# Ready outputs of the first mixer split ahead of the memory projection, the memory projection's weight rests used last in a step, half a projection step ahead of two transposes

## The chip, the cores and the metric

One core of a Trainium2 chip runs the whole kernel. The metric is the device time of one execution in microseconds (us); the median of the runs before the change is 2076.57.

The engines have these names here: PE (TensorE, matmuls and transposes), DVE (VectorE), ACT (ScalarE), POOL (GpSimd) and SP (SyncE, which issues most transfers).

## The reference, cut to what matters

A hybrid encoder of two layers works on 512 positions of 1024 features. Each layer adds half a SwiGLU to its input, then the output of a mixer, then cross-attention to a memory of 256 rows, then half a second SwiGLU. What the change touches:

```
# mixer, layer 0: h @ w_in -> 8 heads with top-k keys (q, k normalised), 4 differential heads
#   logits = q.k + bias, masked; p = softmax; attn = p1 - lam * p2; o = rmsnorm(attn @ v)
# mixer, layer 1: h @ w_in -> 16 heads over a band of 9 chunks of 64
#   p = softmax(q.k + bias); o = p @ v
h = h + concat(o) @ w_out
# cross-attention, 4 heads of 128
k, v = split(rmsnorm(memory) @ mem_wkv)      # memory: 256 x 1024
h = h + softmax(norm(h' @ wq) . norm(k)) @ v @ wo
```

## The kernel before, in words

**Products.** Every fp32 product is made from two parts of each operand: `h`, the value rounded to the format that TensorE reads, and `l`, the rest. Three matmuls then add up: high by high, high by low, low by high. For weights ScalarE makes `wh` (line 161) from the landed `wf`, and VectorE or GpSimd makes `wl` (line 163). Which of the two makes it follows a table of shares: in layer 0's memory projection every second `wl` is GpSimd's, in layer 1's all are VectorE's. There are two buffers each of `wh` and `wl`. For the attention's outputs ScalarE makes `oh` (line 1327) and VectorE the rest `ol` (line 1329).

**Order of TensorE.** TensorE's order is written out by hand: a generator of projections and one of attention are woven together (`weave`, line 79). The attention yields gaps in ns, and the projections yield the cost of each piece; the weave pulls pieces until a gap is filled. The other engines' orders come from a scheduler that knows the dependencies, with some instructions held behind others by `behind` and `issue_after`. PSUM has eight banks: four with the tag `pa` for projections and four with `pb` for attention.

**A mixer.** Six chunks of the input projection come first (`gemm_nat`, matmuls in line 706). Their four banks are copied out by ScalarE (`raw`, line 731) and normalised per head. Then follows the memory projection (`mem_kv`, matmuls in line 1104): eight steps over the features, each of them 12 matmuls into four banks, two for the keys and two for the values. Within a step the banks come one after the other, and each gets `wh*mh`, `wl*mh` and `wh*ml` in a row; after the first two banks and after the last two it yields 1300. Its end empties the banks: keys by ScalarE (line 1110), values by ScalarE (the high part, line 1116) and then VectorE (the rest, line 1117). At last comes the output projection (`out_proj`, matmuls in line 657), which takes four banks of the tag `pa` and works through the outputs in steps of 12 matmuls.

Beside it runs the attention: transposes of queries and keys (lines 766 and 785, split by ScalarE in 775, 789 and 790, and VectorE in 776 and 791), logits (812), the exponentials with bias and maximum (DVE 825, ACT 826), transposes of the probabilities (837, split by ScalarE in 840 and by VectorE in 841 into pz0, pz1 and pz2), values (864 and 920), and the outputs' assembly (868, 869, 873, 874). In layer 0 the differential heads give the first outputs.

**Splitting the outputs.** `mix_out` hands `out_proj` a function `parts(k)`; it makes `oh` and `ol` of output k when it is first asked and the output is ready. It is asked when `out_proj` reaches step k.

**Cross-attention** (`xattn`, line 1163). Queries in line 1254; `soft` makes the logits (1196), the maxima (1199), the exponentials (1204) and their scaling (1211) of a head; `turn` makes eight transposes of a head's probabilities in two banks (1219), each split by ScalarE (1220) into pz0h or pz2h and by VectorE (1221) into pz0l or pz2l; `values` makes six matmuls (1231) and splits their result into `oh` (1234) and `ol` (1236), which are what the output projection of the cross-attention reads (line 657 again).

## Time and profile before

| what | value |
|---|---|
| median of 3 runs | 2076.57 us (2076.25 to 2076.64) |
| the profiled execution | 2077.4 us |
| its span | 2075.6 us |
| mean granted TensorE clock | 0.999 |
| busy: PE | 2045.8 us |
| busy: DVE | 1564.7 us |
| busy: ACT | 1136.6 us |
| busy: POOL | 361.7 us |

The span runs from the first to the last instruction that the profiler shows; the execution's own time is a little longer. A line of the timeline gives start and duration in us, the engine, the line in the kernel, the operation and its output and input; in brackets stands how long the engine was idle ahead of it, and what ended that. A line of the waits gives who waited for whom, the total in us, the number of times and the longest. A line of the windows gives, for a stretch of time, the busy time of PE, its weight loads, DVE, ACT and POOL with their number of instructions, and then the granted clock of TensorE, where 1.00 is full speed.

### The profile page before, as it was taken

The page shows a single profiled execution, that of the slowest core. Times are in us where ns is not written, and L with a number is a line of the kernel's source. Part 1 is how long each engine was busy: PE and PEld are TensorE (multiplying, and loading weights), DVE is VectorE, ACT ScalarE, POOL GpSimd, SP SyncE. Part 2 cuts the span into 40 slices and gives each one's busy share as a digit, 9 for nine tenths or more (in the row PEclk, how much of TensorE's full clock was granted, in tenths as well). Part 3 has the DMA queues.
Part 4 walks back from the last instruction along what each step waited for, and adds up shares of the span by engine and source line. Part 5 has one row for each costly group of instructions (what it writes and reads, how often), then busy time and mean ns, then how long its engine had stood idle before and what let it go on. Part 6 is the DMA issues. An engine that isn't in the chain of part 4 may idle for free.

```text
span 2075.6 us, 32512 instructions
## 1 busy us (share of the span) xinstructions
PE 2045.8 (99%) x12834; PEld 1825.3 (88%) x12834; DVE 1564.7 (75%) x2246; ACT 1136.6 (55%) x1701; POOL 361.7 (17%) x319
## 2 busy tenths in 40 slices
PE   8999999999999999999999999999999999999999
PEld 7989897888788889898989899988888888989997
DVE  8959687699676698685889687685668687958676
ACT  6636354556686565362556354454778566626442
POOL 1101003345431110000020000013453122000000
PEclk9999999999999999999999999999999999999999
DMA  7837545222241166573556466444223324647643
GB/s 218 221 113 193 142 115 180 82 87 82 83 137 61 62 184 172 143 192 113 128 158 176 129 182 164 122 126 149 92 82 125 100 72 141 184 122 182 164 120 94
DMA packets 86121, 279.65 MB, mean 135 GB/s; under 512 B 9680, under 2 KB 12880, under 8 KB 85968
## 3 DMA queue, kind: packets, MB, share of 16 engines
q1 hardware_dynamic: 74448, 235.62, 35.3%
q0 software_dynamic: 11520, 41.95, 11.8%
q8 instruction: 101, 1.65, 0.3%
q14 instruction: 52, 0.43, 0.1%
HBM read 271.24 MB, written 6.29 MB: 134 GB/s over the span
## 4 chain that ended last, share of the span: by engine, by line
PE 86%; DVE 9%; ACT 2%; issue 2%; POOL 1%; DMA 1%; SPq 0%; DVEq 0%; ACTq 0%; POOLq 0%
PE ps_pa L468 26%; PE ps_pa L604 10%; PE ps_pa L706 10%; PE ps_pb L604 10%; PE ps_pb L468 9%; PE ps_pa L657 4%; PE ps_pb L812 2%; PE ps_pa L323 2%; PE ps_pa L1254 2%; PE ps_pb L864 1%; PE ps_pa L1104 1%; PE ps_pb L657 1%; PE ps_pb L837 1%; DVE wl L163 1%; PE ps_pa L1023 1%
## 5 line engine op out<-in xcount | busy, mean ns | idle before, releaser
L161 ACT ACTIVATE wh<-wf 128x1024 fp32r<-128x1024 f32 (+2 forms) x211 | 215.3, 1022 | 345.9 <-PE ps_pa L604 122.1
L163 DVE TENSOR_TENSOR wl<-wf,wh 128x1024 fp32r<-128x1024 f32 (+2 forms) x169 | 200.0, 1188 | 32.5 <-ACT wh L161 29.9
L446 ACT ACTIVATE wh<-s 128x1024 fp32r<-128x1024 f32 x108 | 114.9, 1063 | 111.9 <-PE ps_pa L468 33.6
L525 POOL DMA_DIRECT2D s<-l_ffn_wq x40 | 35.4, 885 | 782.8 <-ACT s L524 739.0
L447 DVE TENSOR_TENSOR wl<-s,wh 128x1024 fp32r<-128x1024 f32 x108 | 132.0, 1222 | 44.3 <-ACT wh L446 40.1
L446 ACT ACTIVATE wh<-wf 128x1024 fp32r<-128x1024 f32 x84 | 89.2, 1062 | 105.9 <-PE ps_pa L468 32.6
L163 POOL TENSOR_TENSOR wl<-wf,wh 128x1024 fp32r<-128x1024 f32 x42 | 101.4, 2415 | 137.6 <-ACT wh L161 135.7
L706 PE MATMUL ps_pa<-wh,xh 128*128 128x512 f32 x384 | 122.8, 401 | 0.1
L706 PE MATMUL ps_pa<-wh,xl 128*128 128x512 f32 x384 | 119.4, 392 | 0.0
L706 PE MATMUL ps_pa<-wl,xh 128*128 128x512 f32 x384 | 119.1, 391 | 0.0
L447 DVE TENSOR_TENSOR wl<-wf,wh 128x1024 fp32r<-128x1024 f32 x84 | 102.5, 1220 | 5.5 <-PE ps_pa L323 3.0
L228 POOL TENSOR_TENSOR acc<-acc,sq 128x512 f32<-128x512 f32 (+1 forms) x37 | 53.0, 1433 | 260.7 <-ACT sq L227 259.7
L614 DVE TENSOR_TENSOR dn<-ps_pa,R 128x512 f32<-128x512 f32 x48 | 33.1, 689 | 83.9 <-PE ps_pa L604 83.5
L604 PE MATMUL ps_pb<-hh,wh 128*128 128x512 f32 x352 | 95.5, 389 | 0.0
L604 PE MATMUL ps_pb<-hl,wh 128*128 128x512 f32 x352 | 95.4, 389 | 0.0
L604 PE MATMUL ps_pb<-hh,wl 128*128 128x512 f32 x352 | 95.4, 389 | 0.0
L604 PE MATMUL ps_pa<-hh,wh 128*128 128x512 f32 x328 | 88.9, 390 | 0.0
L604 PE MATMUL ps_pa<-hl,wh 128*128 128x512 f32 x328 | 88.7, 389 | 0.0
L604 PE MATMUL ps_pa<-hh,wl 128*128 128x512 f32 x328 | 88.6, 389 | 0.0
L614 DVE TENSOR_TENSOR dn<-ps_pb,R 128x512 f32<-128x512 f32 x48 | 33.0, 687 | 71.1 <-PE ps_pb L604 70.7
L706 PEld LDWEIGHTS ps_pa<-wh,xl 128*128 128x128 f32 x384 | 72.5, 189 | 15.9
L706 PEld LDWEIGHTS ps_pa<-wl,xh 128*128 128x128 f32 x384 | 72.4, 188 | 15.8
(377 smaller groups left out, 5853.1 us busy)
## 6 DMA issues: line engine op xcount, KB each, us to landing
wf<-l_ffn_wq SPq DMA_DIRECT2D x120, 512.0 KB, 3.8
s<-l_ffn_wq SPq DMA_DIRECT2D x80, 512.0 KB, 4.4
s<-l_ffn_wq POOLq DMA_DIRECT2D x80, 512.0 KB, 7.4
wf<-l_ffn_wd SPq DMA_DIRECT2D x64, 512.0 KB, 4.1
wf<-l_w_in SPq DMA_DIRECT2D x48, 512.0 KB, 3.3
wf<-l_ffn_wd SPq DMA_DIRECT2D x32, 384.0 KB, 3.1
wf<-l_mem_wkv SPq DMA_DIRECT2D x16, 512.0 KB, 3.3
wf<-l_w_out SPq DMA_DIRECT2D x16, 512.0 KB, 3.3
```

The source lines that it names most:

```text
L161: self.leading = nc.scalar.activation(wh[:, sl], w[:, sl], AF.Copy)
L163: eng.tensor_sub(wl[:, sl], w[:, sl], wh.bitcast(F32)[:, sl])
L228: self.summed = (eng or nc.gpsimd).tensor_add(acc[:, :n], acc[:, :n], sq[:, :n])
L323: nc.tensor.matmul(p, w[a][:, k * P:(k + 1) * P], xs[k][c], start=k == order[0] and a == c == 0, stop=k == order[-1] and a == 1)
L446: self.leading = nc.scalar.activation(h, t, AF.Copy)
L447: self.parted = nc.vector.tensor_sub(l, t, h.bitcast(F32))
L468: self.nc.tensor.matmul(bank[:, sl], w[a][:, o:o + P], xs[k][b], start=first and z == a == b == k == 0, stop=z == a == 1 and k == KB // 2 - 1,
L604: self.nc.tensor.matmul(bank, w[a][:, j * P:(j + 1) * P], h, start=j == a == e == 0, stop=j == nb - 1 and (a, e) == ops[-1])
L614: nc.vector.tensor_mul(t, bank, f.R)
L657: nc.tensor.matmul(banks[dd], a[:, o:o + P], parts(k)[b], start=k == first and a is wh and b == 0, stop=k == last and a is wl)
L706: nc.tensor.matmul(banks[i], xs[k][a][:, i * P:(i + 1) * P], w[b][:, kk * 512:kk * 512 + 512], start=k == a == b == 0, stop=k == KB - 1 an ...
L812: nc.tensor.matmul(bank[:, o:o + n], a, b[:, :n], start=c == 0, stop=c == len(ops) - 1)
```

## The change

It has three parts.

1. In the first mixer, all outputs that are ready at the end of the input projection are split right there, ahead of the memory projection. Their instructions are held behind `self.mark`, the last of the pz rests. For that the function `parts` is made earlier, in `out_parts`, and handed to `mix_out`. The second mixer calls `out_parts` where it called `mix_out`, so its outputs are split as before.
2. In both mixers' memory projections a step has two halves: `wh*mh` and `wh*ml` for all four banks, and then `wl*mh` for all four. It yields 870 three times, after 4, 8 and 12 matmuls, and not 1300 twice, after 6 and 12.
3. In the cross-attention of both layers a gap of 1300 stands ahead of the second head's `turn`, and the gap behind it is 2600, not 3900.

```
-            for i in range(2):
-                for c in range(2):
-                    for n, (a, b) in enumerate(((mh, wh), (mh, wl), (ml, wh))):
-                        nc.tensor.matmul(banks[c][i], a[:, i * P:(i + 1) * P], b[:, c * 512:(c + 1) * 512],
-                                         start=(k == 0 and n == 0), stop=(k == KB - 1 and n == 2))
-                yield 1300
+            for half in (((mh, wh), (ml, wh)), ((mh, wl),)):
+                for i in range(2):
+                    for c in range(2):
+                        for a, b in half:
+                            nc.tensor.matmul(banks[c][i], a[:, i * P:(i + 1) * P], b[:, c * 512:(c + 1) * 512],
+                                             start=k == 0 and a is mh and b is wh, stop=k == KB - 1 and b is wl)
+                    if i or len(half) > 1:
+                        yield 870
...
             s(2, values(0, vp))
+            yield 1300
             turn(es[1])
-            yield 3900
+            yield 2600
...
-    def mix_out(self, src, order, os, mp):
+    def out_parts(self, os):
...
-            o = os[order[k]]
+            o = os[k]
...
+        return parts
+
+    def mix_out(self, src, parts, mp):
...
+            parts = self.out_parts(os)
...
+                with self.behind(self.mark):
+                    for k in range(KB):
+                        parts(k)
                 yield from self.mem_kv(pre, mp)
-                yield from self.mix_out(I[pre + "w_out"], list(range(KB)), os, mp)
+                yield from self.mix_out(I[pre + "w_out"], parts, mp)
```

In the changed kernel lines 1104, 1110, 1116 and 1117 have the numbers 1105, 1112, 1118 and 1119; 1196, 1204, 1211, 1219 to 1221, 1231, 1234 and 1236 are two higher; 1327 and 1329 are 1330 and 1332.

What it does to the order of the instructions shows at three places. The first is VectorE in the first mixer, at the end of the input projection: `qz` and `kz` are rests of queries and keys, `pz` of probabilities, `ol` of an output, `wl` of a weight. Before:

```order
L776 TENSOR_TENSOR qz_3577<-ps_pb,qz_3577 64x512
L791 SCALAR_TENSOR_TENSOR kz0l<-ps_pb,gcol,kz0h 64x512
L1329 TENSOR_TENSOR ol<-x,oh 128x512
L776 TENSOR_TENSOR qz_3578<-ps_pb,qz_3578 64x512
L791 SCALAR_TENSOR_TENSOR kz1l<-ps_pb,gcol,kz1h 64x512
L841 TENSOR_TENSOR pz0l<-ps_pb,pz0h 128x512
L841 TENSOR_TENSOR pz1l<-ps_pb,pz1h 128x384
L841 TENSOR_TENSOR pz2l<-ps_pb,pz2h 128x384
L163 TENSOR_TENSOR wl<-wf,wh 128x1024
```

And now:

```order
L776 TENSOR_TENSOR qz_3577<-ps_pb,qz_3577 64x512
L791 SCALAR_TENSOR_TENSOR kz0l<-ps_pb,gcol,kz0h 64x512
L776 TENSOR_TENSOR qz_3578<-ps_pb,qz_3578 64x512
L791 SCALAR_TENSOR_TENSOR kz1l<-ps_pb,gcol,kz1h 64x512
L841 TENSOR_TENSOR pz0l<-ps_pb,pz0h 128x512
L841 TENSOR_TENSOR pz1l<-ps_pb,pz1h 128x384
L841 TENSOR_TENSOR pz2l<-ps_pb,pz2h 128x384
L1332 TENSOR_TENSOR ol<-x,oh 128x512 x3
L163 TENSOR_TENSOR wl<-wf,wh 128x1024
```

An `ol` has left its place between the two `qz`, and three of them stand in a row behind the last `pz` rest, ahead of the `wl`.

The second place is the end of the memory projection. On TensorE in layer 0, before, the last step's matmuls, the attention's values and transposes, and the first of the output projection (of the values, two of eight are shown):

```order
L1104 MATMUL ps_pa<-wh,mh 128x512
L1104 MATMUL ps_pa<-wl,mh 128x512
L1104 MATMUL ps_pa<-wh,ml 128x512
L864 MATMUL ps_pb<-pz0h,vp 128x512
...
L864 MATMUL ps_pb<-pz2l,vp 128x256
L766 MATMUL ps_pb<-ident,qk 128x128 x4
L785 MATMUL ps_pb<-ident,qk 128x128 x4
L657 MATMUL ps_pa<-oh,wh 128x512
L657 MATMUL ps_pa<-ol,wh 128x512
```

And now:

```order
L864 MATMUL ps_pb<-pz2l,vp 128x256
L766 MATMUL ps_pb<-ident,qk 128x128 x4
L785 MATMUL ps_pb<-ident,qk 128x128 x4
L1105 MATMUL ps_pa<-wh,mh 128x512
L1105 MATMUL ps_pa<-wh,ml 128x512
L1105 MATMUL ps_pa<-wh,mh 128x512
L1105 MATMUL ps_pa<-wh,ml 128x512
L1105 MATMUL ps_pa<-wl,mh 128x512 x4
L657 MATMUL ps_pa<-oh,wh 128x512
L657 MATMUL ps_pa<-ol,wh 128x512
```

Eight matmuls of the last step have moved behind the transposes, the four with `wl` one after the other, and the output projection follows them directly. At the same place in layer 1, ScalarE had these before (`qk` is the copy of a key bank, `vp` the high part of a value bank):

```order
L161 ACTIVATE wh<-wf 128x1024
L1110 COPY qk<-ps_pa 128x512
L1116 ACTIVATE vp<-ps_pa,mem_r 128x4x128
L715 ACTIVATE sq<-qk 128x512
L868 COPY ot<-ps_pb 64x512
L1110 COPY qk<-ps_pa 128x512
L715 ACTIVATE sq<-qk 128x512
L161 ACTIVATE wh<-wf 128x1024
L1116 ACTIVATE vp<-ps_pa,mem_r 128x4x128
```

And now, with the exponentials `e` of a head ahead of them:

```order
L826 ACTIVATE e_16330,rs<-e_16330,m 128x128
L161 ACTIVATE wh<-wf 128x1024
L826 ACTIVATE e_16333,rs<-e_16333,m 128x256
L840 CAST pz0h<-ps_pb 128x512
L826 ACTIVATE e_16336,rs<-e_16336,m 128x384
L840 CAST pz1h<-ps_pb 128x384
L840 CAST pz2h<-ps_pb 128x384
L826 ACTIVATE e_16339,rs<-e_16339,m 128x512
L1112 COPY qk<-ps_pa 128x512
L1118 ACTIVATE vp<-ps_pa,mem_r 128x4x128
L1112 COPY qk<-ps_pa 128x512
L1118 ACTIVATE vp<-ps_pa,mem_r 128x4x128
```

The four instructions that empty the banks stand in one row now, behind the exponentials.

The third place is ScalarE in the cross-attention, at the second head's transposes. Before (`xqh` is a query's high part, `xe` the exponentials of the third head, `pz0h` and `pz2h` the second head's probabilities):

```order
L1173 CAST xqh<-ps_pa 128x512
L1234 CAST oh<-ps_pb 128x512
L1220 CAST pz0h<-ps_pb 128x512
L1177 ACTIVATE sq<-ps_pa 128x512
L1220 CAST pz2h<-ps_pb 128x512
L1204 ACTIVATE xe,xrs<-ps_pb,xm,xf 128x256 x4
```

And now:

```order
L1175 CAST xqh<-ps_pa 128x512
L1236 CAST oh<-ps_pb 128x512
L1179 ACTIVATE sq<-ps_pa 128x512
L1206 ACTIVATE xe,xrs<-ps_pb,xm,xf 128x256 x4
L1222 CAST pz0h<-ps_pb 128x512
L1222 CAST pz2h<-ps_pb 128x512
```

The two casts of probabilities have moved behind the four exponentials.

## The prediction

> **What bounds the kernel now.** I read the page first: busy time of each engine and their shares of the span.

> ```profile
> PE 2045.8 (99%) x12834; PEld 1825.3 (88%) x12834; DVE 1564.7 (75%) x2246; ACT 1136.6 (55%) x1701; POOL 361.7 (17%) x319
> ```

> TensorE is busy for 2045.8 us of the 2075.6 us span. The change takes no matmul and no transpose away, so all it can give or take is time in which TensorE waits, 29.8 us now, or runs at a lower clock. The next view is the list of what TensorE waited for (total, times, longest); these lines touch the changed places, in program order L837 (first mixer), L1104 (memory projection), L1219 (cross-attention) and L657 (output projection).

> ```profile
> PE ps_pb L837 <- DVE qz L776: 2.5, 2, 2.0
> PE ps_pa L1104 <- POOL wl L163: 1.9, 2, 1.0
> PE ps_pb L1219 <- DVE ol L1236: 1.9, 2, 0.9
> ...
> PE ps_pa L1104 <- ACT qk L731: 0.7, 1, 0.7
> PE ps_pa L1104 <- DVE wl L163: 0.5, 1, 0.5
> ...
> PE ps_pa L657 <- DVE vp L1117: 0.3, 1, 0.3
> ```

> That is 7.8 us of waits within reach. Third, the timeline (start, duration, engine, line) says how each arises and what it costs beside the wait itself.

> **Part 1, the early split (first mixer).** The place is the end of the input projection.

> ```profile
> 539.17 2.17 DVE L1329 TENSOR_TENSOR ol<-x,oh 128x512 fp32r<-128x512 f32 x1
> 539.23 0.92 PE L837 MATMUL ps_pb<-ident,e 128*128 128x128 f32 x7
> ...
> 541.37 0.69 DVE L776 TENSOR_TENSOR qz<-ps_pb,qz 64x512 fp32r<-64x512 f32 x1
> ...
> 542.21 0.60 PE L837 MATMUL ps_pb<-ident,e 128*128 128x128 f32 x3 [2.05 <-DVE qz L776]
> ```

> The split rest ol holds VectorE for 2.17 us, qz stands behind it, qz frees the PSUM bank, and the last transposes wait 2.05 us. The windows view has the granted clock (the number ahead of the DMA share) in four stretches of 3.40 us.

> ```profile
> 539.10:542.50 3.40, 1.35 (x13) 1.05 (x11) 3.34 (x4) 2.34 (x4) 1.69 (x1) 1.00 0.20 37
> 542.50:545.90 3.40, 3.40 (x11) 2.73 (x9) 1.97 (x4) 0.48 (x1) 0.00 (x0) 0.50 0.31 122
> 694.00:697.40 3.40, 2.46 (x15) 1.83 (x15) 3.40 (x9) 1.67 (x3) 1.01 (x1) 1.00 0.33 122
> 697.40:700.80 3.40, 3.40 (x18) 2.78 (x17) 1.68 (x7) 2.35 (x9) 0.00 (x0) 1.00 0.00 0
> ```

> After a stretch with 1.35 us of TensorE work in 3.40 the clock was 0.50 for the next 3.40; half of that, 1.70 us, is lost. After 2.46 of 3.40 it stayed at 1.00. So the place costs 2.05 + 1.70 and about 0.15 for the slow first transposes: 3.9 us. With ol moved behind the pz rests, qz can run at 539.17 and ends near 539.9, about when TensorE is through with the first seven transposes (540.0) and wants its bank: wait and clock drop both go, **-3.9** (bounds 0, if DVE finds something else, and -3.9). The moved ols, three of at most 2.17, land in a stretch of the memory projection where the wl on VectorE follows them; it is used last by part 2, so I charge nothing. Without that cover they would cost up to the 2.17 of one.

> **Part 2, weight rests last (memory projection).** Layer 0 first: matmuls of one step, the third of the rows needing wl.

> ```profile
> 557.75 0.39 PE L1104 MATMUL ps_pa<-wh,ml 128*128 128x512 f32 x1
> 557.98 0.39 PE L1104 MATMUL ps_pa<-wh,mh 128*128 128x512 f32 x1
> 559.37 0.50 PE L1104 MATMUL ps_pa<-wl,mh 128*128 128x512 f32 x1 [1.01 <-POOL wl L163]
> 559.71 0.39 PE L1104 MATMUL ps_pa<-wh,ml 128*128 128x512 f32 x1
> ```

> Matmuls start every 0.23 us; here one starts 1.39 after the last and the next 0.34 later, so the stall costs 1.16 + 0.11 = 1.27. There are two such (1.9 in the list of waits), -2.5. With wl used last, 8 matmuls (1.8 us) stand ahead of the first that needs it, against 1: both stalls should go. But TensorE then reaches the next head's softmax earlier, while ScalarE has this in front of that head's last exponential:

> ```profile
> 564.66 1.04 ACT L161 ACTIVATE wh<-wf 128x1024 fp32r<-128x1024 f32 x1
> ```

> Between 0 and 1.27 of the first stall comes back there; I take 0.7, since the 1.04 stands in the way and some of it is covered. Layer 0's steps: **-1.8**.

> The exits are the other side. Until now each bank finished in its own 3 matmuls, the first 9 matmuls ahead of the end; now all four banks finish in the last 4 matmuls, and out_proj (L657), which needs these banks, follows directly. Before, in layer 0, transposes stood between, and L657 started without a wait. Here are its first matmul, what ScalarE runs after the attention's values (L864), and the mean costs of the work that empties the banks (from the groups by form).

> ```profile
> 596.74 0.48 PE L657 MATMUL ps_pa<-oh,wh 128*128 128x512 f32 x1
> ```

> ```profile
> 597.67 0.58 ACT L868 COPY ot<-ps_pb 64x512 f32<-64x512 f32 x1
> 598.28 0.58 ACT L775 CAST qz<-ps_pb 64x512 fp32r<-64x512 f32 x1
> 598.76 0.68 ACT L789 ACTIVATE kz0h<-ps_pb,gcol 64x512 fp32r<-64x512 f32 x1
> 599.46 0.68 ACT L790 ACTIVATE kz0h<-ps_pb,gcol 64x512 fp32r<-64x512 f32 x1
> ```

> ```profile
> L1116 ACT ACTIVATE vp<-ps_pa,mem_r 128x512 fp32r<-128x512 f32 x4 | 2.8, 703 | 0.0
> ...
> L1110 ACT COPY qk<-ps_pa 128x512 f32<-128x512 f32 x4 | 2.4, 598 | 0.5 <-PE ps_pa L1104 0.5
> ```

> ```profile
> 597.16 0.75 DVE L1117 SCALAR_TENSOR_TENSOR vp<-ps_pa,mem_r,vp 128x512 fp32r<-128x512 f32 x1 [0.71 <-ACT vp L1116]
> ```

> Let E be the end of the L864s. The new order has on TensorE 8 transposes (0.8 us), 8 matmuls (1.8), then L657: wanted at E+2.7. On ScalarE it has ot, qz, both kz0h (2.5 by the spacing of the rows), wh (1.04), and only then the first bank's copy (0.6): done E+4.3, a stall of 1.6. Three L657 later (0.7, so at E+5.0) the second bank's copy, behind another qz and a vp (0.58 and 0.70, overlapping a little), is done at E+6.0: 1.0 more. The last bank, by vp on ScalarE and then 0.75 on VectorE, adds 0.1 to 0.2. **+2.8**. Bounds: 0.3 for each exit, if ScalarE stood free, and 4.3 if nothing overlapped.

> Layer 1: the fourth bank's first matmul, which waits for the copy L731 already (0.7), is reached 3 matmuls sooner: **+0.7**. In three places between softmax pieces 4 matmuls stand instead of 6, 0.45 less cover each; 0 to 1.35, and as VectorE and ScalarE run full there I take **+1.1**. The wl wait goes with its slow restart (0.5 + 0.27, the stall above less its wait): **-0.8**. The vp wait (0.3 and the same restart) is counted in the exit: **-0.6**. The exit stands behind a softmax whose rows in before, at the like place, are these (ten transposes at 1587.76; the exponentials, with the durations' least, median and greatest in ns and first and last start; a wh like the one above stands among them):

> ```profile
> 1587.76 1.64 PE L837 MATMUL ps_pb<-ident,e 128*128 128x128 f32 x10
> ```

> ```profile
> L826 ACT ACTIVATE e<-e,m x4: 388/558/740, 1588.2 to 1592.0; 128x128 f32<-128x128 f32 x1, 128x256 f32<-128x256 f32 x1, 128x384 f32<-128x384 f32 x1, 128x512 f32<-128x512 f32 x1
> ```

> From the transposes' start V the last exponential ends at 1592.0 + 0.74 - 1587.76 = V+4.9; in the new order it stands ahead of the first bank's copy, which then ends at V+5.4 (0.6, overlapping a tenth). L657 is wanted at V+2.0 (ten transposes of 0.11, four matmuls): 3.4. The second bank adds 0.3, the last 0.1: **+3.8**. Without a wait on the softmax it would be 0.3, the other bound.

> **Part 3, half a step ahead of the transposes (cross-attention, both layers).**

> ```profile
> 694.07 0.90 PE L1219 MATMUL ps_pb<-ident,xe 128*128 128x128 f32 x4
> 695.91 0.66 PE L1219 MATMUL ps_pb<-ident,xe 128*128 128x128 f32 x4 [0.94 <-DVE ol L1236]
> ```

> ```profile
> 695.17 0.68 DVE L1236 TENSOR_TENSOR ol<-ps_pb,oh 128x512 fp32r<-128x512 f32 x1
> ```

> ```profile
> L1204 ACT ACTIVATE xe<-ps_pb,xm,xf x4: 554/560/563, 697.8 to 699.4; 128x256 f32<-128x256 f32 x4
> ```

> ```profile
> 700.29 1.14 DVE L1211 TENSOR_SCALAR xe<-xe,xrc 128x256 f32<-128x256 f32 x4
> ```

> The second four transposes lose 1.4 us each layer (0.94, and a slow start) because ol, which ends at 695.85, frees their bank. In the new order the six L657 go first, but their second needs that very ol: wanted near 694.3, it loses 1.55. The wait is not hidden, it changes its line: +0.15. And pz0h and pz2h, which stood before the four exponentials on ScalarE, now stand behind them, pz0l and pz2l behind the four scalings on VectorE. The exponentials can move up by 0.5 (VectorE has no pz0l ahead of their maxima), to end at 699.5; pz0h ends 700.1, the scalings 701.0, pz0l (0.68, as ol) 701.65. TensorE wants L1233 at 695.9 + 5 matmuls + 8 transposes + 6 matmuls = 699.3: it waits 0.8 for pz0h, runs two, and waits 1.1 for pz0l. **+2.1** a layer, **+4.2** in all; bounds -2.8 (the old stalls go and nothing comes) and +5.

> **Sum.** -3.9 - 1.8 + 2.8 + 0.7 + 1.1 - 0.8 - 0.6 + 3.8 + 4.2 = +5.5. At each exit the stretch of 3.4 us may hold less work than the 2.46 that kept the clock (3.4 waiting in layer 1; 2.6 with 0.7 of work between in layer 0), yet as windows fall, half the stall can lie in one and half in the next. I count one drop of the two at 1.7, near the 1.35 row: **+7.2**. The profiled execution's own time is 2077.4 (span 2075.6 and 1.8 around it), so 2084.6 there; against the median of 2076.57, **2083.8**.

> [...]

> **Rivals.** *No clock drop* at the exits, as the 694.00 row keeps 1.00 over a stretch with a 0.94 wait: +5.5, 2082.1, chance 0.20. [...] *Two drops*: +8.9, 2085.5, chance 0.13, if both stretches fall like the 539.10 row. *The exits are hidden*, the not-slower case: ScalarE, 55% busy, empties the four banks as they finish. Place: the first L657 of each out_proj. Then 2.8, 3.8 and 1.7 fall away: -1.1, 2075.5. It decides if the first L657 waits under 0.5 in both layers, that is, if wh and the exponentials run ahead of where I put them; against it, their order on ScalarE is fixed and their inputs come as late as TensorE makes them. Chance 0.28, also for mixes of smaller exits and half the cross-attention's price. *All waits go and none come*, in cross-attention too: -3.9 - 2.5 - 0.8 - 0.6 - 2.8 = -10.6, 2066.0; against it stands that ol is needed either way. Chance 0.08. That the change doesn't do what it says is out: the orders show every moved row. The forecast has 0.31.

> **The numbers.** Slower by over 0.2% (4.2 us; about what a measurement of this kernel can tell from no change): 0.31 + 0.20 + 0.13 = 0.64; within: 0.28; faster: 0.08. The range, 2075.0 to 2087.5, takes in the hidden exits and two drops with 2 us of price bounds; the slower cases alone have 2081 to 2087.5.

> **What the changed profile would show.** No L837 wait on qz near 540 and no 0.50 stretch after it; no L1105 wait on wl; L657 waiting for ScalarE's and VectorE's copies (lines 1112, 1118, 1119) for 2 to 4 us in each mixer; in cross-attention L657 waiting on ol for 1 us and more, L1233 on pz0h and pz0l. I am wrong if L657 starts without waits after the memory projection, or if L1233 waits under 0.5.

## The result, and the profile after

The changed kernel takes 2089.30 us (median of 6 runs, 2086.79 to 2090.68), the kernel before 2076.05 (6 runs, 2074.13 to 2076.64): 13 us slower, ratio 1.0065 with a 95% interval of 1.0054 to 1.0076. The forecast had the sign, slower, but 2083.8 us, and its range ended at 2087.5. The profiled execution took 2087.45 us (span 2085.7), 10.05 more than the one before. The profile of the changed kernel (2087.45) is at the fast end of its runs, and the one of the kernel before (2077.4) lies above all six of its own: of the 3.2 us between 10.05 and 13.25, 1.35 come from the profile before and 1.85 from the one after. What may lie behind that comes up with the clock below.

First, TensorE's waits in the changed kernel (total, times, longest):

```profile
PE ps_pa L657 <- ACT qk L1112: 5.3, 3, 3.1
PE ps_pa L657 <- DVE ol L1238: 2.9, 2, 1.4
...
PE ps_pb L1233 <- DVE pz0l L1223: 1.6, 2, 0.8
PE ps_pa L1105 <- ACT qk L731: 1.4, 1, 1.4
PE ps_pb L937 <- POOL orr L248: 1.3, 1, 1.3
...
PE ps_pa L657 <- DVE x L670: 1.2, 1, 1.2
...
PE ps_pb L837 <- DVE m L825: 1.1, 2, 0.6
...
PE ps_pb L812 <- DVE x L869: 1.0, 1, 1.0
```

The memory projection's waits on `wl` are gone, as are those of the cross-attention's transposes (L1219 before) on `ol`, and the one on `qz` fell from 2.5 to 0.4. In their place stand the output projection's waits for the bank copies (L1112), for `ol` and for L670, and waits that the list of before did not have at all: on `orr` (a small factor of the outputs' norm, made by GpSimd), on the maxima `m`, on the attention's sums `x`. TensorE's idle time grew from 29.8 to 39.4 us, its busy time by 0.5.

Both traces hold the same attention work in the same order, so one can ask of each transpose of it how much later it starts in the changed kernel. Read at the stages' ends, this gives a ledger (positive is later; forecasts are the prediction's):

| stage | forecast, us | traces, us |
|---|---|---|
| end of the first input projection (part 1) | -3.9 | -3.84 |
| layer 0, memory and output projection (part 2) | -1.8 + 2.8 | +5.96 |
| layer 0, cross-attention (part 3) | +2.1 | +2.06 |
| layer 1, memory and output projection (part 2) | +4.2 | +5.26 |
| layer 1, cross-attention (part 3) | +2.1 | +2.08 |
| halved clock at the exits | +1.7 | 0 |
| stretches that the change does not touch | 0 | -1.5 |

Four terms hold within 1.1 us. One is far off, layer 0's memory and output projection, by 5.0; the clock's term is off by 1.7 in this execution. The last row adds up small differences, 0.9 of it ahead of the first mixer's end.

### The profile page after: what moved, and what is told of

The parts are those of the page before. It is cut to its first block, busy times and chain, and to the rows that moved or that the text cites. A ratio compares the mean times of both kernels' runs of the same rounds, so it can differ in the third digit from the quotient of the medians.

```text
span 2085.7 us, 32511 instructions
## 1 busy us (share of the span) xinstructions
PE 2046.3 (98%) x12830; PEld 1822.2 (87%) x12834; DVE 1567.3 (75%) x2246; ACT 1136.4 (54%) x1701; POOL 363.1 (17%) x319
## 4 chain that ended last, share of the span: by engine, by line
PE 87%; DVE 9%; ACT 2%; issue 1%; POOL 0%; DMA 0%; SPq 0%; DVEq 0%; ACTq 0%
PE ps_pa L468 26%; PE ps_pa L706 10%; PE ps_pa L604 10%; PE ps_pb L604 10%; PE ps_pb L468 9%; PE ps_pa L657 4%; PE ps_pa L323 3%; PE ps_pb L812 2%; PE ps_pa L1256 2%; PE ps_pa L1105 2%; PE ps_pb L864 1%; PE ps_pb L837 1%; PE ps_pb L657 1%; PE ps_pa L1023 1%; DVE wl L163 1%
## 5 line engine op out<-in xcount | busy, mean ns | idle before, releaser
L161 ACT ACTIVATE wh<-wf 128x1024 fp32r<-128x1024 f32 (+2 forms) x211 | 215.4, 1022 | 344.2 <-PE ps_pa L604 122.0
L163 DVE TENSOR_TENSOR wl<-wf,wh 128x1024 fp32r<-128x1024 f32 (+2 forms) x169 | 199.3, 1184 | 28.9 <-ACT wh L161 26.4
L163 POOL TENSOR_TENSOR wl<-wf,wh 128x1024 fp32r<-128x1024 f32 x42 | 101.5, 2416 | 145.3 <-ACT wh L161 135.5
```

The costliest lines, as they stand in the source:

```text
L161: self.leading = nc.scalar.activation(wh[:, sl], w[:, sl], AF.Copy)
L163: eng.tensor_sub(wl[:, sl], w[:, sl], wh.bitcast(F32)[:, sl])
```

## The experiments

Each of the twelve is timed against the kernel before in the same session; there were four sessions, with medians of 2076.2 to 2076.9 for the kernel before. The table has medians, and the ratio with its interval. A piece of code shows the lines of an edit, with `...` for what is left out, against the changed kernel where nothing else is said.

| kernel | against before, us | ratio, 95% interval |
|---|---|---|
| part 1 alone | -4.4 | 0.9980 (0.9971 to 0.9989) |
| part 2 alone | +11.0 | 1.0057 (1.0044 to 1.0070) |
| part 3 alone | +3.6 | 1.0018 (1.0009 to 1.0027) |
| parts 1 and 2 | +11.0 | 1.0053 (1.0039 to 1.0067) |
| parts 1 and 2, last step as before | +8.2 | 1.0041 (1.0028 to 1.0054) |
| parts 1 and 2, old gaps | +0.8 | 1.0004 (0.9995 to 1.0013) |
| parts 1 and 2, no wl on GpSimd in layer 0's memory projection | +5.9 | 1.0032 (1.0019 to 1.0044) |
| part 1, wl last within half steps, old gaps | +0.6 | 1.0005 (0.9996 to 1.0014) |
| part 1, old order of products, new gaps | +6.6 | 1.0036 (1.0023 to 1.0050) |
| part 1, no wl on GpSimd in layer 0's memory projection | -4.0 | 0.9982 (0.9973 to 0.9990) |
| part 1, every third wl on GpSimd there | -3.6 | 0.9987 (0.9978 to 0.9995) |
| parts 1 and 2, old gaps, products in thirds | +3.1 | 1.0018 (1.0009 to 1.0027) |

My theory after the result: the time is the sum of TensorE's waits, and layer 0's surplus is made of waits that the forecast did not see because longer ones stood in front of them. The rivals: the parts disturb each other; or what costs is the clock.

**Part 1 alone.** The edit is the diff without its pieces in `mem_kv` and `xattn`.

> Part 1 alone, on the kernel before. Theory of the sum of TensorE's waits: the wait of the last transposes on qz (2.05 us) and the halved clock behind it (1.7) go, everything later just moves up by 3.8; the two waits on GpSimd's wl in layer 0 stay: -3.8 us. Rival: the clock falls by chance of where the gap lies and not in every execution, so that only the wait goes: -2.2 us. A second rival: GpSimd's and VectorE's work in the memory projection cannot move up as far, and gives part back: -1 to -2.

It is 4.4 us faster, and in its trace the stage ends 3.8 earlier and nothing after it moves. The theory holds; the second rival falls. The first is right about the clock, though not for this time: in the profile of part 3 alone the same wait on `qz` stands (2.1), and the clock behind it stayed at 1.00.

**Part 2 alone.** The edit is the piece of the diff in `mem_kv`.

> Part 2 alone. Theory of the sum: layer 1 as in the changed kernel, +5.3 us (exit 3.5, the copy L731 0.7, logits and maxima 1.5, against 1.2 of removed waits); layer 0 +2.6 at the exit, +1.3 for the late sums L670, against -2.5 for the wl waits, and +1.5 for the wait on GpSimd's orr that stood hidden behind the wl wait: together +9 us. Rival: the waits on orr and pz0l come only because part 1 brings TensorE earlier; without it they are not there, and the total is +5 to +6.

It is 11.0 slower, more than the expected 9. In the trace layer 0's memory and output projection cost 6.1 us, with part 1 absent, against 5.96 with it. So the new waits in layer 0 do not come from part 1, and that rival falls. The profile also had two stretches of halved clock (0.50 from 541.26 and from 1623.28), one of them at layer 1's exit, where the changed kernel's had none.

**Part 3 alone.** The edit is the piece of the diff in `xattn`.

> Part 3 alone. Theory: 2.1 us more in each layer's cross-attention, as the traces of before and after stand to each other there (1.28 to 3.35 and 8.14 to 10.22 late): +4.2 us. Rival: the price comes from what the memory projection hands over late, so that alone it costs under 1 us.

+3.6 us; in its trace each cross-attention costs 2.1. The theory holds. Around the wait on `qz` in the first mixer, where nothing is changed, this trace gains 1.56 on the one before: that is what the missing drop of the clock is worth (the mean granted clock is 1.000 here and 0.999 before).

**Parts 1 and 2.** The edit is the diff without its piece in `xattn`.

> Parts 1 and 2, without part 3. Theory of the sum: +11.5 less 4.2 = +7.3 us against before; it should lie 4.2 under the changed kernel. Rival, that the parts interact: the difference to the changed kernel is not that of part 3 alone, by more than 1.5 us.

+11.0, and not +7; it lies 2.2 under the changed kernel, where part 3 alone costs 3.6; the rival asked for a difference of more than 1.5 and so is not met, if barely. In the trace most of the surplus is the clock: the windows of this profile show three halved stretches, each behind a stretch with little work (the wait on `orr` is longer too, 2.4 and not 1.3).

```profile
554.49:557.90 3.41, 1.40 (x11) 1.24 (x11) 2.20 (x4) 0.00 (x0) 3.41 (x3) 1.00 0.34 113
557.90:561.31 3.41, 3.41 (x11) 2.38 (x10) 2.52 (x10) 2.10 (x7) 3.41 (x3) 0.50 0.60 233
595.46:598.87 3.41, 1.25 (x4) 0.77 (x5) 1.95 (x3) 3.36 (x6) 2.37 (x1) 1.00 0.06 25
598.87:602.28 3.41, 3.41 (x9) 2.54 (x9) 2.44 (x4) 2.77 (x5) 0.00 (x0) 0.50 0.45 154
1619.45:1622.86 3.41, 1.03 (x4) 0.55 (x4) 2.71 (x6) 3.41 (x10) 0.54 (x2) 1.00 0.58 198
1622.86:1626.27 3.41, 3.41 (x8) 2.72 (x9) 2.40 (x6) 1.51 (x3) 0.75 (x1) 0.50 0.00 0
```

The same exits stand in the changed kernel's profile, where the clock stayed at full speed. In stretches of the same length, laid as the last section describes, the 3.1 us wait of layer 1 falls half into one and half into the next:

```profile
1615.94:1619.35 3.41, 1.82 (x12) 1.29 (x11) 2.48 (x7) 3.39 (x10) 0.53 (x2) 1.00 0.52 148
1619.35:1622.76 3.41, 1.85 (x7) 1.23 (x8) 2.40 (x6) 3.41 (x8) 0.54 (x2) 1.00 0.49 156
1622.76:1626.17 3.41, 3.41 (x19) 2.80 (x18) 1.90 (x5) 1.27 (x3) 1.56 (x2) 1.00 0.00 0
```

Between the transposes on both sides of layer 1's exit this kernel loses 6.12 us and the changed one 4.61: a drop is 1.5 us. So the same exit costs 1.5 more in one execution than in another, and three drops make 4.5. By the medians part 1's gain of 4.4 does not show when part 2 is there (+11.0 with and without it), though the trace has it, 3.8 us at its place. The three drops can hide it; whether they do so in the unprofiled runs stays open.

**The exits, the last step in the old order.**

```
+            if k == KB - 1:
+                for i in range(2):
+                    for c in range(2):
+                        for a, b in ((mh, wh), (mh, wl), (ml, wh)):
...
+                    yield 1300
+                break
```

> Parts 1 and 2 with the last step of the memory projection in the old order and with the old two gaps: its first two banks are full 6 matmuls ahead of the end and stand in their own piece. Theory, that the exits' price is that all four banks fill in the last four matmuls, just ahead of the output projection: the waits of the first L657 (1.6 + 1.0 in layer 0, 3.2 in layer 1) fall to under 1 us together, the late sums L670 (1.3) go as well, and with the long waits the halved clock: 7 to 9 us less than with both parts, +2 against before. Rival, that the bank copies are late because of what stands ahead of them on ScalarE (wh, casts, exponentials), whatever the order of the banks: no more than 2 us less.

+8.2, only 2.8 under parts 1 and 2: nearer to the rival. The pieces of the first seven steps had shifted the weave already, so that in layer 0 six matmuls of the last step still ran straight into the output projection, and the list of waits has the exits under another name:

```profile
PE ps_pa L657 <- DVE vp L1127: 3.4, 2, 2.1
```

So in layer 0 it is not enough that two banks fill early. In layer 1 even other work did not do: ten transposes stood between the last product and L657, but on ScalarE the last bank's `vp` had exponentials and a `wh` ahead of it, and on VectorE (L1127) a `wl` of 2.11 us, and TensorE waited 2.05 for it. That is close to the rival's account.

**The old gaps with the new order of products.**

```
-                    if i or len(half) > 1:
-                        yield 870
...
+            for n, (i, c, a, b) in enumerate(todo):
...
+                if n % 6 == 5:
+                    yield 1300
```

> Parts 1 and 2, with the weight rests last as in part 2, but with the old two gaps of 1300 after 6 and 12 matmuls. The four banks still fill in the last four matmuls; but attention's values and transposes stand between them and the output projection, as before the change. Theory, that the place of the pieces and not the order of the products makes the price: L657 waits under 0.5 us in each layer, the wl waits stay away, about -2 to 0 against before. Rival, that the four banks' late filling costs it: +4 or more against before.

+0.8: of the 11.0 us some 10 are gone, although the four banks still fill in the last four matmuls of a step. In this kernel attention's work stands ahead of the output projection again (values and transposes in layer 0, logits in layer 1), and L657 no longer waits for a copy. The place of the pieces was the larger price; the rival, late filling, falls. But with part 1's -4.4 in it the kernel should have been 4 faster: the order of products costs 5 by itself (and the expected -2 to 0 was missed). In its trace the two mixers' memory and output projections cost 4.0 and 3.0. In layer 0 the largest part is a wait of 1.9 on `orr`, with a drop of the clock behind it (0.50 from 557.41). In layer 1 it is waits for the copy L731, the exponentials, the maxima and `ml`; the last of these is shown here, on TensorE and then on VectorE, around the one place where TensorE had waited for `wl` before:

```profile
1600.61 0.39 PE L1103 MATMUL ps_pa<-wh,mh 128*128 128x512 f32 x1
1601.76 0.50 PE L1103 MATMUL ps_pa<-wh,ml 128*128 128x512 f32 x1 [0.76 <-DVE ml L1100]
```

```profile
1599.24 1.23 DVE L163 TENSOR_TENSOR wl<-wf,wh 128x1024 fp32r<-128x1024 f32 x1 [0.35 <-ACT wh L161]
1600.49 0.69 DVE L776 TENSOR_TENSOR qz<-ps_pb,qz 64x512 fp32r<-64x512 f32 x1
1601.22 0.48 DVE L1100 SCALAR_TENSOR_TENSOR ml<-mem,cols,mh 128x256 fp32r<-128x256 f32 x1
```

`wl` is wanted last now, but VectorE makes it first, and `ml`, which was third in a step, is wanted second. The wait for `wl` has become one for `ml`.

**The old order with the new gaps.** This is the fourth field of the square of old and new order, old and new gaps; the edit is shown against part 1 alone.

```
                         nc.tensor.matmul(banks[c][i], ...
...
+                        if (6 * i + 3 * c + n) % 4 == 3:
+                            yield 870
-                yield 1300
```

> Part 1, the old order of products, and of part 2 only the gaps: three of 870 after 4, 8 and 12 matmuls. The pieces then stand as in the changed kernel: the last 8 matmuls of layer 0's memory projection just ahead of the output projection, in layer 1 the last 4. Theory, that the place of the pieces is nearly the whole price of part 2: +8 to +11 us against part 1 alone, so +4 to +7 against before, with L657 waiting for the bank copies. Rival, that it takes the weight rests last as well: under +3 against part 1 alone.

+6.6 against before, 11.0 over part 1 alone. So by the medians the gaps cost 11.0 with the old order of products and 10.2 with the new one; the order costs 5.2 with the old gaps and 4.4 with the new ones. The two add up to the 15.4 between part 1 alone and parts 1 and 2. In the traces, with one drop of 1.5 taken out, they do not quite: the two stages cost 8.5 with the new gaps alone, 5.5 with the new order alone and 11.2 with both (the changed kernel). The larger price is the gaps' in either count; how much of the medians is the clock stays open. The list of waits shows that the `wl` waits stay and the exits come:

```profile
PE ps_pa L657 <- DVE vp L1118: 2.6, 2, 1.9
...
PE ps_pa L657 <- ACT qk L1111: 2.1, 2, 1.2
PE ps_pa L1104 <- POOL wl L163: 2.1, 2, 1.1
...
PE ps_pa L657 <- DVE x L670: 1.2, 1, 1.2
```

**GpSimd.** The share that sets which `wl` GpSimd makes in layer 0's memory projection is changed, `WS[7] = 0`.

> Parts 1 and 2, and in layer 0's memory projection every wl is VectorE's, none GpSimd's. Theory, that the wait of L937 on orr (1.3 to 2.4) and VectorE's long ml and ol (1.7, 2.7) come from GpSimd's wl that stands ahead of orr and beside them: the orr wait falls under 0.3, pz0l and the maxima come in time, 2 to 3 us less than with both parts. Rival, that orr is late by GpSimd's own chain of norms (3.2 + 1.0 ahead of it): the wait stays over 1 us; and VectorE, with 1.24 more for each of four wl, is late elsewhere: no gain.

+5.9, 5 less than parts 1 and 2, where 2 to 3 was expected. In the traces layer 0's stage costs 2.5 here and 6.0 in the changed kernel, neither with a drop in it, and 0.9 comes back in the cross-attention as a wait on the sums `acc` (L255): 2.6, which is what was expected. The wait on `orr` fell from 2.4 to 0.3, as the theory wants, so the rival (GpSimd's own chain of norms) falls:

```profile
PE ps_pb L937 <- POOL orr L248: 0.3, 1, 0.3
```

In the changed kernel GpSimd has `wl` straight ahead of `orr`:

```profile
552.26 2.41 POOL L163 TENSOR_TENSOR wl<-wf,wh 128x1024 fp32r<-128x1024 f32 x1
554.61 1.02 POOL L248 TENSOR_TENSOR orr<-ov,mhalf 128x4 f32<-128x4 f32 x1
```

```profile
555.69 0.65 PE L937 MATMUL ps_pb<-ident,orr 128*128 128x128 f32 x4 [1.32 <-POOL orr L248]
```

Before, TensorE waited 1.0 for that `wl`, and `orr` was made during its next matmuls:

```profile
559.29 1.00 POOL L248 TENSOR_TENSOR orr<-ov,mhalf 128x4 f32<-128x4 f32 x1
```

Now it does not ask for `wl` so soon, comes to L937 earlier, and waits 1.3 for the instruction behind.

The other two waits of layer 0's steps, 0.6 on `pz0l` and 0.6 on `m`, hang on GpSimd's `wl` as well. In the changed kernel two instructions of VectorE that stand ahead of `pz0l` and of the maxima ran beside one (563.17 to 565.57 and 582.62 to 585.02):

```profile
564.16 1.69 DVE L1100 SCALAR_TENSOR_TENSOR ml<-mem,cols,mh 128x256 fp32r<-128x256 f32 x1 [0.22 <-ACT mh L1098]
582.83 2.74 DVE L1332 TENSOR_TENSOR ol<-x,oh 128x512 fp32r<-128x512 f32 x1
```

Without GpSimd's share the same two took 0.49 and 0.68, and both waits are gone from layer 0; before, `ml` and `ol` at the like places took 0.47 and 0.69, with no `wl` of GpSimd beside them.

**wl last within half steps.** The edit is shown against part 1 alone.

```
-                    for n, (a, b) in enumerate(((mh, wh), (mh, wl), (ml, wh))):
+                for half in (((mh, wh), (ml, wh)), ((mh, wl),)):
+                    for c in range(2):
+                        for a, b in half:
```

> Part 1, and within each half step of 6 matmuls the weight rest last (wh*mh and wh*ml of two banks, then wl*mh of these two), with the old gaps of 1300 and so with the old order of pieces. wl is wanted 3 matmuls (0.68 us) later than before. Theory: the two wl waits of layer 0 shrink by 0.68 each and that of layer 1 goes, but L937's wait on orr comes in place of the first: about 1 us less than part 1 alone, -5 against before. Rival: whatever the wl wait gives, the next instruction that depends on VectorE or GpSimd takes: no difference to part 1 alone.

+0.6, which is 5 worse than part 1 alone: both expectations missed. I had counted only what `wl` gives. The waits have moved to `orr` (1.3), to `ml` (0.8), and the one for the copy L731 has grown to 0.9.

```profile
PE ps_pb L937 <- POOL orr L248: 1.3, 1, 1.3
...
PE ps_pa L1105 <- ACT qk L731: 0.9, 1, 0.9
PE ps_pa L1105 <- DVE ml L1100: 0.8, 1, 0.8
```

**Thirds.**

```
+            todo = [(i, c, a, b) for a, b in ((mh, wh), (ml, wh), (mh, wl)) for i in range(2) for c in range(2)]
```

> Part 1 with the old two gaps, and each step in thirds: wh*mh for all four banks, then wh*ml, then wl*mh. So the memory's rest ml is wanted as the fifth matmul of a step (part 2: second; before: third), wl as the ninth as in part 2. Theory, that part 2's order pays partly because it wants ml before wl while VectorE makes wl first: the waits on ml (0.8 in layer 1, 0.3 to 0.6 in layer 0) go, 1 to 2 us less than with parts 1 and 2 and the old gaps, so about -1 against before; those on orr, the copy L731 and the maxima stay, so it does not reach part 1 alone (-4). Rival, that ml's wait is one more place where VectorE is late whatever is asked for first: its 0.8 shows at the next instruction, no difference.

+3.1, 2 more than with halves, where 1 to 2 less was expected (about -1 against before). The waits for `ml` are gone, as the theory said, and layer 0's stage costs 1.3 us in the trace. But the fourth bank is now reached with the fourth matmul of the first step, and its old content, the raw copy of L731, is not out yet:

```profile
PE ps_pa L1103 <- ACT qk L731: 3.1, 1, 3.1
```

That wait took two halved stretches with it, one after the other (the mean granted clock of this profile is 0.998, before 0.999). Here a first step that opens all four banks with its first four matmuls pays 3.1 at its start, where the halves paid 1.4.

**Faster still?** Part 1 with fewer or no `wl` on GpSimd.

> Part 1 alone, and in layer 0's memory projection every wl is VectorE's. Theory: both waits on GpSimd's wl (1.27 us each with the slow restart) go, and orr comes 2.4 us earlier, so nothing takes their place: 2 to 2.5 us less than part 1 alone, -6 against before. Rival: VectorE has four more wl of 1.24 us in that stretch and gives it back: no difference to part 1 alone.

> Part 1 alone, and in layer 0's memory projection every third wl is GpSimd's, not every second. Theory: a wait on GpSimd's wl is there only where its wl stands behind the head norms on GpSimd (the two places of before); with fewer of them one or both go: 0 to 2.5 us less than part 1 alone. Rival as for the kernel without any: no difference.

-4.0 and -3.6, beside -4.4 for part 1 alone: no difference that can be told. The `wl` waits go (1.9 to 0 and to 0.9), and a wait of 0.7 on the sums `acc` (L255) comes in their place in both, with 0.6 on `pz0l` in the one without GpSimd; the rival holds. Part 1 alone and these two, with 2072.3 to 2072.6 us, are the fastest kernels here, faster than before and after.

## Why the prediction was wrong, by its own steps

- **The bound** (TensorE 99% busy; only waits and clock can change) held: of the 10.1 us by which the profiled span grew, 9.6 are idle time of TensorE. The waits named here, with their slow restarts (0.34 from the first start behind a wait to the next, 595.42 to 595.76, where 0.23 is usual), account for 5.0 of layer 0's 5.96 and 4.5 of layer 1's 5.26; the rest lies in small delays that are not assigned.
- **Part 1, -3.9:** the traces say -3.84, the kernel with it alone -4.4. The cover that I named, that the moved rests cost nothing behind the pz rests, held. Its halved stretch was priced at 1.70; measured, a drop is worth 1.5 to 1.56.
- **Part 2, layer 0's steps, -1.8: this step failed.** It said that both `wl` stalls go and 0.7 of the first returns, 1.27 at most. Both went. But the waits of 1.3 on `orr`, 0.6 on `pz0l` and 0.6 on `m` came, each with its slow restart: with 0.3 more on pz1l together 3.3 us. So the steps cost about 1 us more (3.3 less 2.3 for the two stalls) where 1.8 less was forecast. All three waits hang on `wl` instructions of GpSimd: `orr` is the next instruction behind the one that TensorE used to wait for, and VectorE's `ml` and `ol` grew long beside two others; with VectorE making every `wl` these waits fall to 0.3, 0 and 0. I had followed the instruction that was no longer waited for, and not the next one of the same engine that TensorE meets, nor what runs beside it. And I had not asked what the new order wants earlier: `ml`.
- **Layer 0's exit, +2.8:** the waits were 1.6 and 1.0 with their restarts, for the copies of the first and the second bank as worked out; ScalarE's row was the one that I had read:

```profile
595.42 0.50 PE L657 MATMUL ps_pa<-oh,wh 128*128 128x512 f32 x1 [1.45 <-ACT qk L1112]
...
597.22 0.50 PE L657 MATMUL ps_pa<-oh,wh 128*128 128x512 f32 x1 [0.83 <-ACT qk L1112]
```

  What was left out, put at nothing, is the output projection's own half-way point, the wait of 1.2 on the sums L670 with its restart (1.4): with the pieces shifted, L657 opens its next four banks before VectorE has emptied the last. VectorE was not busy, though, and eight matmuls and eight transposes of the attention stood between on TensorE. In VectorE's order the sums stand behind L869, which needs those very matmuls:

```profile
617.70 0.68 DVE L869 TENSOR_TENSOR x<-ps_pb,ot 64x512 f32<-64x512 f32 x1 [3.11 <-ACT ot L868]
618.31 2.46 DVE L670 TENSOR_TENSOR x<-ps_pa,xr 128x512 f32<-128x512 f32 x4
```

  Before, two of the four sums were done by 614.1 and the last started at 616.56, ahead of that L869 (619.16). Every kernel with the new gaps has the wait, none with the old ones.
- **Layer 1, +4.2:** measured 5.26. The copy L731 grew by 0.68 (3 matmuls, as said), the exit cost 3.5 (forecast 3.8), the covers between the softmax pieces 1.5 (1.1), and the two waits that went gave 1.2 (1.4). In the working of the exit the last exponential ends at V+5.0 (1592.0 + 0.74 - 1587.76), not V+4.9. The first L657 and the exponential that ScalarE had ahead of the copy:

```profile
1620.82 0.51 PE L657 MATMUL ps_pa<-oh,wh 128*128 128x512 f32 x1 [3.06 <-ACT qk L1112]
```

```profile
1619.46 0.74 ACT L826 ACTIVATE e<-e,m 128x512 f32<-128x512 f32 x1
...
1620.18 0.59 ACT L1112 COPY qk<-ps_pa 128x512 f32<-128x512 f32 x1
```

- **Part 3, +4.2:** measured 2.06 and 2.08, and +3.6 alone. Even the places are those of the working: `ol` for the second L657, then pz0h, then pz0l. The sizes agree partly by luck: the last two waits are 0.45 and 0.78, not 0.8 and 1.1, and their slow restarts, which were not priced, make up for it:

```profile
697.20 0.50 PE L657 MATMUL ps_pa<-ol,wh 128*128 128x512 f32 x1 [1.45 <-DVE ol L1238]
...
701.33 0.73 PE L1233 MATMUL ps_pb<-pz0h,vp 128*128 128x512 f32 x2 [0.45 <-ACT pz0h L1222]
702.84 0.50 PE L1233 MATMUL ps_pb<-pz0l,vp 128*128 128x512 f32 x1 [0.78 <-DVE pz0l L1223]
```

- **The clock, +1.7:** one drop at two exits was counted. The profiled execution had none; those of five other kernels with the new gaps had none, one, one, two and three in the two output and memory projections. It differs from execution to execution for the same wait (behind the 3.1 of layer 1's exit it was 0.50 in the profile of parts 1 and 2 and 1.00 in the changed kernel's), and so it belongs to a mean, not to a sum. The profile before had one drop (behind the wait on `qz`) and the one after had none, so drops of 1.5 can account for much of the 3 us between the profile's difference and the medians'. That they do is not shown, since unprofiled runs have no clock row by stretch.
- **The rivals:** no drop (+5.5) described the clock of the profiled execution and missed the waits; hidden exits fell with the first row of the waits. None of them had the mechanism that decided, a wait behind the wait. The sign, slower, came from the exits and the cross-attention, which were right; it was not luck.

## What to carry to other kernels

When a change lets the bound engine skip a wait, follow the late engine on to its next instruction: here TensorE skipped 1.0 on `wl` and then waited 1.3 on `orr`, the next of GpSimd, and in the kernel with the old gaps 0.8 on `ml`, the operand that had become the early one. In a woven order look where the last piece of a stage ends: work of another kind between the last product into a bank and the next use of that bank can hide its emptying (with the old gaps L657 waits for no copy), and smaller gaps can take it away without one product being moved (with the old order and the new gaps L657 waits 4.7 for copies and rests). Look also at what stands ahead of the emptying on its own engine: if that needs the work in between, the work hides nothing (the 1.2 on L670, behind L869). A chain of waits at 99% busy is worth more as a list of who is late than as a sum that one may subtract from.

## What the runs showed of the hardware

```profile
554.00:557.41 3.41, 1.49 (x12) 1.24 (x11) 2.19 (x4) 0.00 (x0) 3.41 (x3) 1.00 0.34 113
557.41:560.82 3.41, 3.41 (x9) 2.35 (x9) 2.52 (x10) 2.56 (x8) 3.41 (x3) 0.50 0.60 233
```

Those that were not had 1.78 and more: 1.78 in the profile of the old order with new gaps (from 1614.06; its mean granted clock is 1.000), 1.82 and 1.85 in the changed kernel's rows above, 1.96 and 2.05 in those of part 2 alone (from 595.90 and 1578.90). So in these profiles the measured cases part between 1.49 and 1.78 of 3.41 us, and where the grid fell on a wait went with the clock behind it: of layer 1's wait of 3.1 us 2.4 lay in one stretch with parts 1 and 2 (1.03 of work, then 0.50), and half in each of two in the changed kernel (1.82 and 1.85, then 1.00). The wait of 2.05 us on `qz` was followed by a drop in two of the profiles that hold it (before, part 2 alone) and not in that of part 3 alone. This can be one reason why the kernel before ran between 2074.1 and 2079.1 us in one session while its order never changed; that it is the reason is not shown, and one drop of 1.5 does not make 5.

Two operations of VectorE took longer beside GpSimd's `wl`. In the changed kernel `ml` took 1.69 us at 564.16, during the `wl` from 563.17 to 565.57, and `ol` 2.74 at 582.83, during the one from 582.62 to 585.02. At 1601.22 in the kernel with the old gaps `ml` took 0.48, and at 1601.48 before, where GpSimd was busy for 0.00 from 1599.60 to 1603.00, 0.49.
